# One layer of a hybrid block on one core: first-load blocks in unused tiles, the last gates' modulation inside the second norm, a branch projection ahead of two gates

## The chip, the core and the metric

The kernel runs on one core of a Trainium2 chip. The core has a matrix engine (TensorE, PE; its weight loads are shown as PEld), a vector engine (VectorE, DVE), an engine for activation functions (ScalarE, ACT), a general engine (GpSimd, POOL) and an engine that here only issues DMA transfers (SyncE, SP). They run side by side, each through its own list of instructions in order, and wait for one another by semaphores. The metric is the time on the device of one execution, in microseconds.

## What is computed

All in float32, batch 1: 512 latent tokens x, 256 context tokens ctx, width 1024. A vector c and a fixed vector c_ctx give six modulation vectors (shift, scale and gate for two halves of the layer) by one matrix of 1024 x 6144.

```python
mod_x = silu(c) @ w_mod + b_mod;  mod_c = silu(c_ctx) @ w_mod + b_mod
sh1, sc1, g1, sh2, sc2, g2 = split(mod, 6)          # latent ones; sh1, sc1 for the context too
h = rmsnorm(x, norm1_g) * (1 + sc1) + sh1           # context likewise
f, u, g = split(h @ w_in, [512, 1024])              # Fourier group, recurrent group, gate branch
u = dwconv(u)                                       # width 4, along rows
for d in (forward, backward):                       # context first, the latents go on from its end
    r, i = sigmoid(u @ w_a + b_a), sigmoid(u @ w_x + b_x)    # the "gates"
    a = exp(-8 * r * softplus(-lam))                # the "decays"
    s = scan(s * a + sqrt(1 - a * a) * (i * u))
rx = (s_fwd + s_bwd) * gelu(g)
mx = concat(rmsnorm(fourier(f)), rmsnorm(rx)) @ w_out
x = x + g1 * mx
h2 = rmsnorm(x, norm2_g) * (1 + sc2) + sh2
x = x + g2 * peer(h2)      # product-key retrieval over 16384 experts, top 16 of 8 heads
return rmsnorm(x, final_norm_g)
```

## The kernel before, in words

Tokens lie along the free dimension, channels along the 128 partitions. A float32 product is made of three matmuls of rounded halves (`mm3`, L131): high by high, high by low, low by high. Weights arrive in tiles `raw` of 128 x 2048 (1 MB), which are split by `split_w` (L126): ACT copies the high half (`whi`), DVE, or POOL where it says so, subtracts for the low half (`wlo`). There are two `raw` tiles and two more with the mark "U", and the same for the split weights; a load on SP waits until a tile of its kind is free. The other work tiles of the first part are 35 equal buffers (`bt`, 128 x 768), and the PSUM tiles are five "ps", two "pa" and one "pm".

PE, ACT and DVE follow the order in which the code is written, from the start of the kernel to the end of the first part: `in_order` (L83) chains all their instructions. On SP the loads of the opening are chained in the same way; POOL's order and SP's later one are the scheduler's, which may also place work of the second part early.

**Modulation.** The matrix comes in 24 loads (`mod_load`, L180); load n is multiplied by `mod_mm(n)` (L211), eight instructions into the PSUM tile "pm", which `cc32` (the two vectors) feeds as stationary operand. Loads 0 to 7 are reordered on the host so that 0 to 3 make the scale and 4 to 7 the shift of the first norm. `mod_first(z)` (L226) ends such a half: ACT copies the sums, PE turns them onto partitions by eight matmuls, DVE adds the bias. Loads 8 to 15 and 16 to 23 are each ended by `mod_out` (L239) in the same way; the last ones hold sc2 (`mods[:, 32:40]`) and g2 (`mods[:, 40:48]`). g2 is first needed late in the second part.

**Opening** (L183 to L335). SP loads x, blocks 0 to 3, the context, the first u weights, blocks 4 to 7, more weights. ACT squares the rows, PE sums them with ones (`mean_squares`, L256), `rsqrt` (L148) makes the root; blocks 0 to 3 give the scale, blocks 4 to 7 the shift. Then the u projection begins.

**Recurrence** (L465 to L538). For each of four channel blocks: convolution, `gates` (four products of the gate weights, ACT's sigmoids), `decays` (exponential, tanh, then a2 = a * a on POOL, L409, and a DVE instruction), `scans`. `gate_branch(k)` (L441) is the projection of the gate branch, 24 matmuls and a copy. `mod_cols(w)` (L458) loads block 8 + w and multiplies block 7 + w. After `gates(3)` follow `mod_cols(3)`, the Fourier weights' loads (L500), their splits, `mod_cols(4)` and (5), `decays([2])`, `gate_branch(3)` and the Fourier projection `f_mm`.

**Output loop** (L663 to L691). Eight blocks `out_mm(k)` of 24 matmuls; the first four take the Fourier half, the last four the recurrent half `mr`. `rec_norm` (L619) makes mr: a multiplication by the root on POOL (L621), ACT's high half and DVE's low half (`scaled_split`, L567). `out_add` (L634) evacuates; for k < 4 DVE makes a product (L641) and POOL adds it to x (L642), else DVE does both (L638). Each turn also multiplies one modulation block, 16 to 23, and `mod_out(2)` ends them at k = 7.

**Second norm** (L692 to L729). Squares of x are summed by PE (`x2_sums`), `rsqrt`, then new pools are opened where the first part's were: A2 from sc2, and for each of eight blocks a DVE product, ACT's high half and DVE's low half (`h2h`, `h2l`), which the query projection of the second part takes.

Of the kernel before, what the change touches and what calls it, by code (L numbers as in the profile page):

```python
# [14 lines left out]
AF = mybir.ActivationFunctionType  # L15
ALU = mybir.AluOpType

P = 128
# [3 lines left out]
ND = 8  # L22
# [29 lines left out]
def build(tc, xT, ctxT, c2t, vecs, wm, wu, wf, wg, wgate, wo, wq, keys, u, v, urow, vrow,  # L52
          dft, c64, sel, eye, out, dbg=None):
    nc = tc.nc
# [110 lines left out]
    def bt(dt=F32, n=L):  # L165
        return bp.tile([P, n], dt, tag="b", name="b")
# [7 lines left out]
    gel2 = p1c.tile([P, 1024], F32, name="gel2")  # L174
    cc32 = cpool.tile([P, ND, 32], F32, name="cc32")
    V.memset(cc32, 0.0)
    xn = [bt() for d in range(ND)]
    rawm = {}

    def mod_load(n, st=""):  # L180
        rawm[n] = load(wm[n // 8, n % 8], st)

    for d in range(ND):  # L183
        nc.sync.dma_start(x2[d], xT[d])
# [3 lines left out]
        nc.sync.dma_start(xn[d][:, :C], ctxT[d])  # L188
    rawu = {0: load(wu[0], cuts=2)}
    for n in range(4, 8):  # L190
        mod_load(n, ("U", "")[n % 2])
    rawu[1] = load(wu[1], "U")
    graw = load(wgate)
    in_order(first_load, (nc.sync.engine,))
# [15 lines left out]

    def mod_mm(n):  # L211
        t = rawm.pop(n)
        if n < 8:

            m, first, final = -1 - n // 4, n % 4 == 0, n % 4 == 3
            ds = [2 * (n % 4) + j // 2 for j in range(4)]
        else:
            m, first, final = n // 8, n % 8 == 0, n % 8 == 7
            ds = [n % 8] * 4
        if first:  # L220
            modp[m] = pst("pm")
        for j in range(4):
            PE.matmul(modp[m][32 * j:32 * j + 32], cc32[:, ds[j]], t[:, j * 512:(j + 1) * 512],
                      start=first, stop=final)

    def mod_first(z):  # L226

        sb = bt(F32, 512)
        act(sb, modp[-1 - z], AF.Copy)
        pT = pst("pa", 32)  # L230
        for b in range(4):
            PE.matmul(pT[:, 4 * b:4 * b + 4], sb[:, b * P:(b + 1) * P], vec[:, V_SEL2:V_SEL2 + 4], start=True, stop=True)
        pv = pT[:, :16].rearrange("p (b j z) -> p z j b", b=4, j=2)
        o = 8 - 8 * z
        for k, mm in enumerate((mods, modc)):
            V.tensor_tensor(mm[:, o:o + 8].rearrange("p (j b) -> p j b", j=2), pv[:, k],
                            vec[:, V_BMOD + o:V_BMOD + o + 8].rearrange("p (j b) -> p j b", j=2), op=ALU.add)

# [16 lines left out]

    def mean_squares(src, n, ss, ds):  # L256
        for d in ds:
            sq = bt()
            act(sq[:, :n], src[d], AF.Square)
            if n == T:  # L260
                if d % 2 == 0:
                    even = sq
                    continue
                V.tensor_tensor(sq[:, :n], sq[:, :n], even[:, :n], op=ALU.add)
            PE.matmul(ss[:, :n], ones, sq[:, :n], start=(d < 2 if n == T else d == 0), stop=(d == ND - 1))
# [20 lines left out]

    for n in range(4):
        mod_mm(n)
    mod_first(0)
    A1 = cpool.tile([P, 2, ND], F32, name="A1")  # L290
    for z, mm in enumerate((mods, modc)):
        V.scalar_tensor_tensor(A1[:, z], mm[:, 8:16], 1.0, vec[:, V_N1:V_N1 + 8], op0=ALU.add, op1=ALU.mult)
# [12 lines left out]
    wpu = [split_w(rawu[0], h) for h in range(2)]  # L305
    mod_mm(6)
    mod_mm(7)
    mod_first(1)

    parts = ((sc, modc), (sx, mods))  # L310

# [88 lines left out]
    def decays(ks):  # L400
        for k in ks:
            for dr in range(2):
                o = 4 * dr + k
                r = rr[k, dr]
                a = aa[k, dr] = bt()
                tact(a, r, AF.Exp, scale=n8[:, o:o + 1])
                tact(r, r, AF.Tanh, scale=z8[:, o:o + 1])
                a2 = bt()
                G.tensor_tensor(a2, a, a, op=ALU.mult)  # L409
                V.scalar_tensor_tensor(r, a2, 1.0, r, op0=ALU.add, op1=ALU.mult)  # L410

    def scans(ks):
# [78 lines left out]
    scans([0, 1])  # L491
    mod_cols(2)
    gate_branch(2)
    gates(2)
    gates(3)
    mod_cols(3)
# [17 lines left out]
    mod_cols(4, "U")  # L514
    mod_cols(5, "U")
    decays([2])
    gate_branch(3)
    f_mm(0, f0)
    f0 = f_weights(2)
    decays([3])  # L520
# [97 lines left out]

    def rec_norm(k):  # L619
        rx = hsum[k][:, C:]  # L620
        G.tensor_tensor(rx, rx, r, op=ALU.mult)  # L621
        mr.append(scaled_split(rx, vec[:, V_LG + k:V_LG + k + 1]))

    def out_mm(k, wp, ms):
# [38 lines left out]
    for k in range(8):  # L663
        psk[k] = out_mm(k, wpo[k], Ys if k < 4 else mr)
        if k == 1:
            ssf, ssr = pst("pa"), pst("pa")
            PE.matmul(ssf, ones, Y0, start=True, stop=True)
            PE.matmul(ssr, ones, sqr, start=True, stop=True)
            rF = bt(F32, 512)
            rsqrt(rF, bt(F32, 512), ssf, 512)  # L670
            r = bt(F32, 512)
            rsqrt(r, bt(F32, 512), ssr, 512)
            out_add(0, psk[0], rF)
        if k:
            out_add(k, psk[k], rF if k < 4 else None)
        if k > 4:
            x2_sums(k - 5)
        if k + 4 < 8:
            wpo[k + 4] = out_weights(k + 4)
        if 0 < k < 3:  # L680
            rec_norm(2 * k - 2)
            rec_norm(2 * k - 1)
        if k < 7:
            mod_cols(9 + k, "U")
        if k == 5:
            raw0 = load(wq[0])
        if k == 7:
            mod_mm(23)
            mod_out(2)
        if k == 6:  # L690
            wpq = [split_w(raw0, p, V) for p in range(2)]  # L691
    x2_sums(3)  # L692
    rsqrt(rstd2, bt(F32, 512), ss2[0], 1024)
    in_order(start, (PE.engine, S.engine, V.engine))
    if "x2" in dbg:
        for d in range(ND):
# [25 lines left out]
    for d in range(ND):  # L722
# [5 lines left out]
        V.scalar_tensor_tensor(lo, xn, shift, hi.bitcast(F32), op0=ALU.add, op1=ALU.subtract)  # L728
        h2.append((hi, lo))  # L729

    pt0.close()
    X2d = dpool.tile([ND, P, T], F32, name="X2d")
    for d in range(ND):
# [482 lines left out]
def prep(i):  # L1216
    a = {}
    a["xT"] = i["x"][0].T.reshape(ND, P, T)
    a["ctxT"] = i["ctx"][0].T.reshape(ND, P, C)
    cols = lambda z: z.reshape(-1, P).T  # L1220
    a["vecs"] = np.concatenate([cols(z) for z in (
        i["b_mod"][0], i["norm1_g"][0], i["norm2_g"][0], i["final_norm_g"], i["conv_w"][0],
        i["conv_b"][0], i["lru_b_a"][0], i["lru_b_x"][0], i["lru_lambda"][0],
        i["fourier_out_g"][0], i["lru_out_g"][0])]
                               + [np.eye(P, dtype=np.float32).reshape(P, 4, 32)[:, :, :2].reshape(P, 8)]
                               + [np.eye(P, dtype=np.float32).reshape(P, 2, 2, 32)[..., :2].sum(1).reshape(P, 4)], 1)
    a["c2t"] = np.stack([i["c"][0], i["c_ctx"]]).reshape(2, ND, P).transpose(2, 1, 0)
    wm = np.array(i["w_mod"][0].reshape(ND, P, 3, 2048).transpose(2, 0, 1, 3))
    wm[0] = (i["w_mod"][0][:, :2048].reshape(4, 2, P, 2, 1024)[:, :, :, ::-1]
             .transpose(3, 0, 2, 1, 4).reshape(ND, P, 2048))  # L1230
    a["wm"] = wm
    w = i["w_in"][0]
    st = lambda m: m.reshape(ND, P, 2, 2, P).transpose(2, 1, 3, 0, 4).reshape(2, P, 2048)
    a["wf"] = w[:, :512].reshape(2, 4, P, 512).transpose(0, 2, 1, 3).reshape(2, P, 2048)
    a["wu"] = st(w[:, 512:1024])
    a["wg"] = st(w[:, 1024:])
    gt = np.zeros((P, 2, 2, 2, 2, P), np.float32)
    for g, n in enumerate(("lru_w_a", "lru_w_x")):
        z = i[n][0].reshape(2, 2, 2, 2, 64, 64)
        for s in range(2):  # L1240
            gt[64 * s:64 * s + 64, :, :, g, :, 64 * s:64 * s + 64] = z[:, :, :, s].transpose(3, 1, 0, 2, 4)
    a["wgate"] = gt.reshape(P, 2048)
    a["wo"] = (i["w_out"][0].reshape(2, 4, P, 2, 4, P).transpose(0, 3, 2, 4, 1, 5)
               .reshape(4, P, 2048))
    a["wq"] = i["peer_w_q"][0].reshape(ND, P, 8, 2, P).transpose(2, 1, 3, 0, 4).reshape(8, P, 2048)
    a["keys"] = i["peer_sub_keys"][0].transpose(0, 3, 1, 2).reshape(8, P, 256)
    a["u"] = i["peer_u"][0].reshape(P, 64, 2, ND, P).transpose(1, 4, 2, 3, 0).reshape(64, P, 2048)
    a["v"] = (i["peer_v"][0].reshape(P, NG, JG, 4, 2, P).transpose(1, 3, 0, 4, 2, 5)
              .reshape(NG * 4, P, 2048))
    a["urow"] = i["peer_u"][0]  # L1250
    a["vrow"] = i["peer_v"][0]
    t = np.arange(T)[:, None]
    k = np.arange(256)[None]
    ang = 2 * np.pi * ((t * k) % T) / T
    z = np.stack([np.cos(ang), np.sin(ang)]).astype(np.float32)
    z[1, :, 0] = 1.0 - 2.0 * (np.arange(T) % 2)
    a["dft"] = z.reshape(2, 4, P, 256).transpose(2, 0, 1, 3).reshape(P, 2048)
    m = np.arange(64)
    ang = 2 * np.pi * ((m[:, None] * m[None]) % 64) / 64
    nrm = 1.0 / np.sqrt(512.0 * 64.0)  # L1260
    bd = np.zeros((2, P, P))
    for s in range(2):
        bd[0, 64 * s:64 * s + 64, 64 * s:64 * s + 64] = np.cos(ang) * nrm
        bd[1, 64 * s:64 * s + 64, 64 * s:64 * s + 64] = np.sin(ang) * nrm
    a["c64"] = np.stack([np.stack(hilo(bd[0])), np.stack(hilo(bd[1]))]).transpose(2, 0, 1, 3)
    a["sel"] = consts_sel()
    a["eye"] = np.eye(P, dtype=np.float32)
    return {n: np.ascontiguousarray(z) for n, z in a.items()}
# [30 lines left out]
```

## Time and profile before

| | |
|---|---|
| Runs | 1470.49 us median of 3 (1469.91 to 1470.79) |
| Profiled execution | 1473.89 us; its span, from first to last instruction, 1472.1 us |
| Busy share of the span | PE 94%, PEld 87%, DVE 84%, ACT 42%, POOL 46% |
| Mean granted clock of PE | 0.976 of full speed |

The first part, from the opening to the second norm, is the first sixth of the span. A row of the timeline gives the start and the length in us, the engine, the line, the operation, the tiles (written <- read), shapes, how often, and in brackets how long the engine stood idle before and what ended that. SPq is SP issuing a DMA. A merged row of several instructions (x4) gives the time from the first start to the last end. L70 is the line of the helper for activations, L115 that of the loads, L123 that of the low halves, L132 to L134 are `mm3`; the tiles tell them apart. "b" is any of the 35 buffers.

### The profile page before, as it was taken

Reading aid. Unit: us, or ns where it says so; the run is one execution under the profiler, and the core shown is the slowest. Engines: PE = TensorE matmul, PEld = TensorE weight load, DVE = VectorE, ACT = ScalarE, POOL = GpSimd, SP = SyncE. Lnnn points to the kernel's source line nnn. Section 1 sums busy time; section 2 is a strip of 40 time slices with the busy share of each in tenths; the row PEclk is TensorE's granted clock in tenths of the full one; section 3 lists DMA queues with packets and bytes.
Section 4 is the critical chain, followed back from the end, with each engine's and each line's share of the span. In section 5 each row is a group of like instructions: output and inputs, shape, how many; then the busy total and the mean of one; then the engine's idle time right before and its main releaser. Section 6 shows DMA issues by size and latency. Waiting matters only on the chain. (4 is left out here: it accounts for less than half of the span.)

```text
span 1472.1 us, 22568 instructions
## 1 busy us (share of the span) xinstructions
PE 1390.7 (94%) x8569; PEld 1287.3 (87%) x8569; DVE 1235.5 (84%) x2186; ACT 613.4 (42%) x881; POOL 680.6 (46%) x460
## 2 busy tenths in 40 slices
PE   6898998999989999999999999999999999899995
PEld 2775765888869999999999999999999999899995
DVE  5577875699988998488998989999898989899973
ACT  4467633443334656433333432424334343233351
POOL 0044163566430000365765757576675766545412
PEclk8899999999999999999999999999999999999998
DMA  9433446331226999999999998999999999999901
GB/s 336 159 114 143 172 172 237 116 132 62 78 88 222 314 304 307 347 371 367 400 361 416 343 388 336 405 365 399 397 365 364 406 351 414 392 410 398 391 32 55
DMA packets 130189, 420.61 MB, mean 286 GB/s; under 512 B 10400, under 2 KB 59808, under 8 KB 106016
## 3 DMA queue, kind: packets, MB, share of 16 engines
q1 hardware_dynamic: 83520, 251.03, 45.9%
q0 software_dynamic: 46560, 168.14, 29.8%
q8 instruction: 67, 1.10, 0.3%
q14 instruction: 42, 0.34, 0.1%
HBM read 385.41 MB, written 33.69 MB: 285 GB/s over the span
## 5 line engine op out<-in xcount | busy, mean ns | idle before, releaser
L70 ACT ACTIVATE whi<-raw 128x1024 fp32r<-128x1024 f32 x296 | 312.6, 1059 | 608.5 <-PE ps_pa L133 296.5
L123 DVE TENSOR_TENSOR wlo<-raw,whi 128x1024 fp32r<-128x1024 f32 x266 | 328.9, 1239 | 61.5 <-ACT whi L70 47.6
L132 PE MATMUL ps_pa<-h2h,whi 128*128 128x352 f32 x1024 | 335.1, 327 | 4.8 <-ACT act L70 4.8
L134 PE MATMUL ps_pa<-h2h,wlo 128*128 128x352 f32 x1024 | 334.3, 326 | 0.6 <-DVE wlo L123 0.6
L133 PE MATMUL ps_pa<-h2l,whi 128*128 128x352 f32 x1024 | 334.4, 327 | 0.0
L1086 POOL DMA_INDIRECT row<-vrow,eidx x128 | 196.2, 1533 | 131.6 <-DVE oacc L1107 93.5
L1086 POOL DMA_INDIRECT row<-urow,eidx x128 | 196.5, 1535 | 117.0 <-DVE row L1093 59.9
L133 PE MATMUL ps_ps<-wl,whi 128*128 128x352 f32 x640 | 207.5, 324 | 0.0
L134 PE MATMUL ps_ps<-wh,wlo 128*128 128x352 f32 x640 | 207.2, 324 | 0.2 <-DVE wlo L123 0.2
L132 PE MATMUL ps_ps<-wh,whi 128*128 128x352 f32 x640 | 206.6, 323 | 0.0
L132 PEld LDWEIGHTS ps_pa<-h2h,whi 128*128 128x128 f32 x1024 | 193.7, 189 | 6.9 <-ACT act L70 5.6
L134 PEld LDWEIGHTS ps_pa<-h2h,wlo 128*128 128x128 f32 x1024 | 193.3, 189 | 1.8 <-DVE wlo L123 0.9
L133 PEld LDWEIGHTS ps_pa<-h2l,whi 128*128 128x128 f32 x1024 | 193.5, 189 | 0.9
L1093 DVE SCALAR_TENSOR_TENSOR row<-row,hrow 128x1024 f32<-128x1024 f32 x128 | 154.1, 1221 | 33.4 <-DMA row<-urow,eidx 31.7
L1107 DVE SCALAR_TENSOR_TENSOR oacc<-row,gw,oacc 128x1024 f32<-128x1024 f32 x127 | 162.8, 1282 | 11.0 <-DMA row<-vrow,eidx 9.8
L134 PEld LDWEIGHTS ps_ps<-wh,wlo 128*128 128x128 f32 x640 | 120.6, 188 | 0.5 <-DVE wlo L123 0.5
L133 PEld LDWEIGHTS ps_ps<-wl,whi 128*128 128x128 f32 x640 | 120.5, 188 | 0.0
L132 PEld LDWEIGHTS ps_ps<-wh,whi 128*128 128x128 f32 x640 | 120.4, 188 | 0.0
L123 POOL TENSOR_TENSOR wlo<-raw,whi 128x1024 fp32r<-128x1024 f32 x30 | 72.0, 2402 | 84.8 <-ACT whi L70 56.9
L133 PE MATMUL ps_pa<-wl,whi 128*128 128x352 f32 x256 | 83.0, 324 | 0.0
L134 PE MATMUL ps_pa<-wh,wlo 128*128 128x352 f32 x256 | 82.8, 323 | 0.0
L132 PE MATMUL ps_pa<-wh,whi 128*128 128x352 f32 x256 | 82.7, 323 | 0.0
(299 smaller groups left out, 2606.7 us busy)
## 6 DMA issues: line engine op xcount, KB each, us to landing
raw<-u SPq DMA_DIRECT2D x64, 1024.0 KB
raw<-v SPq DMA_DIRECT2D x64, 1024.0 KB
raw<-wm SPq DMA_DIRECT2D x24, 1024.0 KB
Gd<-stg SPq DMA_DIRECT2D x22, 1024.0 KB
gt<-Gd SPq DMA_DIRECT2D x16, 1408.0 KB
raw<-wq SPq DMA_DIRECT2D x8, 1024.0 KB
Ad<-act SPq DMA_DIRECT2D x10, 704.0 KB
act<-Ad SPq DMA_DIRECT2D x10, 704.0 KB
```

Of the source, the lines that this page charges most:

```text
L70: return S.activation(o, i, f, **kw)
L123: lo_ins[0] = (lo_eng or V).tensor_tensor(dst[1], src, dst[0].bitcast(F32), op=ALU.subtract).ins
L132: PE.matmul(ps, a[0], b[0], start=start, stop=False)
L133: PE.matmul(ps, a[0], b[1], start=False, stop=False)
L134: PE.matmul(ps, a[1], b[0], start=False, stop=stop)
L1086: G.indirect_dma_start(out=t, out_offset=None, in_=tab, in_offset=bass.IndirectOffsetOnAxis(ap=e[:, s:s + 1], axis=0))
L1093: ins = V.scalar_tensor_tensor(t, t, 1.0, hr, op0=ALU.mult, op1=ALU.mult, accum_out=dt[:, s:s + 1])
L1107: ins = V.scalar_tensor_tensor(o, t, g[:, s:s + 1], o, op0=ALU.mult, op1=ALU.add)
```

## The change

Loads 4 to 7 get tiles of their own: sixteen buffers of the 35, of which 512 columns are used, are set aside before all others (`ahead`), and each load is four DMAs of 128 x 512 (`mod_load_b`). The squares of the first norm, which used such buffers, go into slices of `gel2`, a tile that is used later. Loads 16 to 23 are reordered like 0 to 7: 16 to 19 make sc2, 20 to 23 make g2. Loads 16 to 18 are multiplied in turns 0 to 2 of the output loop; 19 is multiplied and turned in turn 3; 20 to 23 are loaded in turns 3 and 4 into buffers of the 35, multiplied and turned behind the sums of the second norm, and their bias is added behind the eight blocks of h2. `mod_first` is split into `half_turned` (copy and turn) and `half_biased`. `gate_branch(3)` stands ahead of `gates(2)` and `gates(3)`. The squares of the decays and the multiplications in `rec_norm` go from POOL (G) to DVE (V).

```diff
+    ahead = {n: [bt()[:, :512] for j in range(4)] for n in range(4, 8)}
     xn = [bt() for d in range(ND)]
...
     def mod_load(n, st=""):
-        rawm[n] = load(wm[n // 8, n % 8], st)
+        t = load(wm[n // 8, n % 8], st)
+        rawm[n] = [t[:, j * 512:(j + 1) * 512] for j in range(4)]
+    def mod_load_b(n):
+        rawm[n] = ahead.get(n) or [bt()[:, :512] for j in range(4)]
+        for j, t in enumerate(rawm[n]):
+            nc.sync.dma_start(t, wm[n // 8, n % 8, :, j * 512:(j + 1) * 512])
...
     for n in range(4, 8):
-        mod_load(n, ("U", "")[n % 2])
+        mod_load_b(n)
...
     def mod_mm(n):
-        if n < 8:
+        if n < 8 or n >= 16:
...
-            PE.matmul(modp[m][32 * j:32 * j + 32], cc32[:, ds[j]], t[:, j * 512:(j + 1) * 512],
-                      start=first, stop=final)
+            PE.matmul(modp[m][32 * j:32 * j + 32], cc32[:, ds[j]], t[j], start=first, stop=final)
-    def mod_first(z):
+    def half_turned(n):
         sb = bt(F32, 512)
-        act(sb, modp[-1 - z], AF.Copy)
+        act(sb, modp[-1 - n // 4], AF.Copy)
         pT = pst("pa", 32)
         for b in range(4):
             PE.matmul(pT[:, 4 * b:4 * b + 4], sb[:, b * P:(b + 1) * P], vec[:, V_SEL2:V_SEL2 + 4], start=True, stop=True)
+        return pT[:, :16].rearrange("p (b j z) -> p z j b", b=4, j=2)
+    def half_biased(pv, o, outs):
+        for k, mm in enumerate(outs):
             V.tensor_tensor(mm[:, o:o + 8].rearrange("p (j b) -> p j b", j=2), pv[:, k],
...
     def mean_squares(src, n, ss, ds):
-            sq = bt()
+            sq = gel2[:, d % (1024 // n) * n:][:, :n]
...
-    mod_first(0)
+    half_biased(half_turned(3), 8, (mods, modc))
...
-    mod_first(1)
+    half_biased(half_turned(7), 0, (mods, modc))
...
-                G.tensor_tensor(a2, a, a, op=ALU.mult)
+                V.tensor_tensor(a2, a, a, op=ALU.mult)
...
     gate_branch(2)
+    gate_branch(3)
     gates(2)
     gates(3)
...
     decays([2])
-    gate_branch(3)
     f_mm(0, f0)
...
-        G.tensor_tensor(rx, rx, r, op=ALU.mult)
+        V.tensor_tensor(rx, rx, r, op=ALU.mult)
...
-        if k < 7:
+        if k < 3:
             mod_cols(9 + k, "U")
+        if k == 3:
+            mod_mm(19)
+            half_biased(half_turned(19), 32, (mods,))
+        if k in (3, 4):
+            mod_load_b(14 + 2 * k)
+            mod_load_b(15 + 2 * k)
         if k == 5:
             raw0 = load(wq[0])
-        if k == 7:
-            mod_mm(23)
-            mod_out(2)
...
     rsqrt(rstd2, bt(F32, 512), ss2[0], 1024)
+    for n in range(20, 24):
+        mod_mm(n)
+    last_gates = half_turned(23)
     in_order(start, (PE.engine, S.engine, V.engine))
...
         h2.append((hi, lo))
+    half_biased(last_gates, 40, (mods,))
...
-    wm[0] = (i["w_mod"][0][:, :2048].reshape(4, 2, P, 2, 1024)[:, :, :, ::-1]
-             .transpose(3, 0, 2, 1, 4).reshape(ND, P, 2048))
+    for m, o in ((0, -1), (2, 1)):
+        wm[m] = (i["w_mod"][0][:, 2048 * m:2048 * m + 2048].reshape(4, 2, P, 2, 1024)[:, :, :, ::o]
+                 .transpose(3, 0, 2, 1, 4).reshape(ND, P, 2048))
```

## Rows read from the trace of the kernel before

**Rows 1.** The waits of PE, 0 to 270 us: total, times, longest, in us.
```profile
PE ps_ps L132 <- ACT b L70: 8.8, 3, 7.3
```

**Rows 2.** The timeline of PE, 22 to 46 us: start, length, operation, [idle before].
```profile
25.41 6.72 PE L265 MATMUL ps_ps<-b,ones 128*128 128x256 f32 x16
...
35.00 1.06 PE L223 MATMUL ps_pm<-raw,cc 128*32 128x512 f32 x8 [1.02 <-DMA raw<-wm]
39.69 1.94 PE L223 MATMUL ps_pm<-raw,cc 128*32 128x512 f32 x8 [3.62 <-DMA raw<-wm]
```

**Rows 3.** The timeline of DVE, 24 to 46 us.
```profile
37.69 2.36 DVE L123 TENSOR_TENSOR wlo<-raw,whi 128x1024 fp32r<-128x1024 f32 x2
44.25 0.17 DVE L236 TENSOR_TENSOR mods<-ps_pa,vec 128x8 f32<-128x8 f32 x1 [4.21 <-PE ps_pa L232]
```

**Rows 4.** Busy time by stretch; the last two columns: DMA share, GB/s.
```profile
25.00:32.50 7.50, 7.50 (x23) 5.63 (x27) 5.79 (x12) 1.40 (x5) 0.00 (x0) 0.56 1.02 425
32.50:35.00 2.50, 1.49 (x16) 0.26 (x8) 2.19 (x6) 2.04 (x3) 0.00 (x0) 1.00 0.58 246
```

**Rows 5.** The DMA packets of 8 to 10 us.
```profile
DMA packets 404, 0.84 MB, mean 422 GB/s; under 512 B 49, under 2 KB 49, under 8 KB 385
```

**Rows 6.** The timeline of ACT, 100 to 136 us.
```profile
108.80 0.94 ACT L70 ACTIVATE b<-b,n 128x768 f32<-128x768 f32 x1 [1.64 <-DVE b L410]
...
117.16 1.28 ACT L70 ACT_TABLE_LOAD   x1 [0.18 <-DVE b L419]
118.45 3.33 ACT L70 ACTIVATE b<-ps_ps,vec 128x256 f32<-128x256 f32 x7
...
133.23 2.01 ACT L70 ACTIVATE whi<-raw 128x1024 fp32r<-128x1024 f32 x2 [5.19 <-DMA raw<-wf]
```

**Rows 7.** The timeline of DVE, 103 to 114 us.
```profile
104.24 0.96 DVE L410 SCALAR_TENSOR_TENSOR b<-b 128x768 f32<-128x768 f32 x1 [2.31 <-POOL b L409]
...
112.19 1.22 DVE L123 TENSOR_TENSOR wlo<-raw,whi 128x1024 fp32r<-128x1024 f32 x1
```

**Rows 8.** Busy time of PE on tile ps_pa in one stretch: us (instructions), granted clock.
```profile
103.40:109.20 5.80, 5.74 (x24) 1.00 0.89 347
```

**Rows 9.** The timeline of SP's DMA issues, 100 to 136 us.
```profile
128.37 1.19 SPq L115 DMA_DIRECT2D raw<-wf  x2
```

**Rows 10.** The timeline of DVE, 196 to 224 us.
```profile
202.66 2.72 DVE L641 SCALAR_TENSOR_TENSOR b<-ps_ps,mods,b 128x512 f32<-128x512 f32 x4
205.30 1.22 DVE L123 TENSOR_TENSOR wlo<-raw,whi 128x1024 fp32r<-128x1024 f32 x1
206.43 3.48 DVE L570 SCALAR_TENSOR_TENSOR b<-b,vec 128x512 fp32r<-128x512 f32 x2
```

**Rows 11.** The timeline of POOL, 200 to 224 us.
```profile
205.31 2.34 POOL L642 TENSOR_TENSOR x<-x,b 128x512 f32<-128x512 f32 x1
```

**Rows 12.** The timeline of ACT, 196 to 224 us.
```profile
212.35 0.72 ACT L70 ACTIVATE b<-b,vec 128x512 fp32r<-128x512 f32 x1 [2.23 <-POOL b L621]
212.98 1.04 ACT L70 ACTIVATE whi<-raw 128x1024 fp32r<-128x1024 f32 x1
```

**Rows 13.** The timeline of PE around 213 and from 240 to 253 us.
```profile
213.08 1.06 PE L223 MATMUL ps_pm<-raw,cc 128*32 128x512 f32 x8
...
242.21 1.06 PE L244 MATMUL ps_pa<-vec,b 128*128 128x8 f32 x8 [0.89 <-ACT b L70]
...
251.76 1.22 PE L132 MATMUL ps_ps<-h2h,whi 128*128 128x512 f32 x2 [5.82 <-ACT h2h L70]
```

**Rows 14.** The timeline of DVE, 244 to 250 us.
```profile
249.71 0.17 DVE L713 TENSOR_SCALAR A<-mods 128x8 f32<-128x8 f32 x1
```

**Rows 15.** The waits of SP, 195 to 262 us.
```profile
SPq L833 <- DVE h2l L728: 15.2, 1, 15.2
```

**Rows 16.** Busy time by stretch; third column from the right: granted clock.
```profile
250.00:251.00 1.00, 0.00 (x0) 0.00 (x0) 0.96 (x3) 0.01 (x1) 0.61 (x1) 0.50 0.00 0
256.00:257.00 1.00, 1.00 (x4) 0.78 (x3) 1.00 (x3) 0.93 (x2) 0.00 (x0) 0.59 0.00 0
```

More of the change, by code (lines that the diff above doesn't have):

```diff
@@ L232, in mod_first @@
             PE.matmul(pT[:, 4 * b:4 * b + 4], sb[:, b * P:(b + 1) * P], vec[:, V_SEL2:V_SEL2 + 4], start=True, stop=True)
-        pv = pT[:, :16].rearrange("p (b j z) -> p z j b", b=4, j=2)
-        o = 8 - 8 * z
-        for k, mm in enumerate((mods, modc)):
+        return pT[:, :16].rearrange("p (b j z) -> p z j b", b=4, j=2)
+    def half_biased(pv, o, outs):
+        for k, mm in enumerate(outs):
             V.tensor_tensor(mm[:, o:o + 8].rearrange("p (j b) -> p j b", j=2), pv[:, k],
```

## The prediction, made before the change was run

> **What bounds the kernel now.** I read the page first, then the waits of TensorE (PE) over the first 270 us, because only code of that stretch changes. PE has work for 94% of the span, so a microsecond counts only if it shortens PE's path. Its longest wait there is for ScalarE (ACT), 7.3 us once before the gates [rows 1]; the blocks of the first modulation load cost it up to 3.62 us at a time [rows 2], the second norm 5.82 [rows 13]. Then I read each stretch in order of time: its rows on every engine, its DMA rate and its granted clock. Behind the norm nothing is edited, and I carry any shift through unchanged. The sum is made in the profiled execution (span 1472.1 us, 1473.89 us with what lies around it); the median of the runs shown is 1470.49 us, 3.4 us less, and I apply the difference to that.
>
> **Opening.** Before, the last of the eight blocks reaches PE at 39.69 us, while the seventh was there at 35.00 [rows 2]. The DMA engines moved 425 GB/s up to 32.5 us and only 246 in the next 2.5 us [rows 4]: the eighth load had no free tile yet. With tiles of its own its megabyte follows the seventh's at 425 GB/s, 1.05 MB / 0.425 = 2.5 us, and reaches PE at about 37.5. It comes in quarters, so only the last quarter's multiplication is then left: I take 0.5 of the 1.94 us row. That is 38.0 against 39.69 + 1.94 = 41.63. The copy, the turn and the bias behind it shift with it. VectorE (DVE) is busy with the low halves of the weights until 37.69 + 2.36 = 40.05 and did the bias at 44.25 [rows 3]; it would now do it at 44.25 - 3.6 = 40.6, not held by them. Gain **3.6 us**; the bounds are 4.2 (DVE the limit) and the loss of rival 3.
>
> Quarters have rows of 2 KB. So have the x loads, and at 8 to 10 us, when 336 of 404 packets are between 2 and 8 KB, the rate is 422 GB/s [rows 5], with several transfers in flight. The Trainium skill (SBUF — State Buffer, The DMA setup-cost knee) puts one 256 KiB transfer at 224 GB/s and one of 1 MiB at about 341, for a fixed cost that each pays; it speaks against the cut. The 422 disagrees as long as transfers overlap; by the page's figure the opening would lose, as in rival 3.
>
> The squares of the first norm now go through two slots of a tile that is unused there (four for the context), so a square waits for the sum that read its slot. Bound: a 256-wide sum takes 6.72 / 8 = 0.84 us [rows 2], a 512-wide one twice that at the same clock, so some 3 us later in all at most. Cover: the multiplications by that root stand behind the bias of the first four blocks anyway. I take nothing; without the cover it is up to 3 us. The new tiles and the reordered weights cost nothing on the chip.
>
> **Decays and the branch projection.** Eight squares of the decays go from GpSimd (POOL) to DVE. A 768-wide operation costs DVE 0.96, and it stood idle 2.31 us before that row, waiting for POOL [rows 7]: no cost. ACT's 1.64 us stop at 108.80 [rows 6] goes, so what follows its exponentials comes 1.7 us sooner. The projection of branch 3 (24 matmuls, 5.74 us as its twin in [rows 8], 0.24 each) now runs inside PE's 7.3 us wait. Its second weight half, ready at 112.19 + 1.22 = 113.4 [rows 7], is ready at 111.7; 22 matmuls later it is 117.0. ACT evacuates it in its written order before the sigmoids: copy 0.6 (under the 0.72 of [rows 12]), table load 1.28, sigmoids at 118.9 against 118.45 [rows 6]. PE is now warm and starts the 48 gate matmuls (half of them 512 wide, half 256) at 117.0: 24 x 0.24 + 24 x 0.12 = 8.6, end 125.6. Before, they ended about one pass before 128.37 [rows 9], at 127.3.
>
> What is late next is the Fourier weights. Their load is issued at 128.37, when the modulation pass behind the gates frees a tile [rows 9]; ACT sits 5.19 us idle until they land at 133.23 [rows 6]. Before, the projection filled that for PE; now nothing does. The load moves only with the gates, 1.7 to 2.3 us. PE's new idle stretch of 4 to 5 us may halve its clock: in the norm it stands at half (1.2 of 2.4 GHz) after 4 us without work and is back only at about 256.8, 5 us after PE restarts [rows 13, 16], which loses 2.5 us. Sum: **gain 0.5 us** (bounds: gain 2.3, loss 0.8).
>
> **Output loop.** Modulation passes 20 to 23 (1.06 us each [rows 13]) leave the loop, 4.0 us of PE. In exchange pass 19 is turned inside the loop, at k = 3: PE does pass 19 (213.08 to 214.1 [rows 13]), waits for ACT's copy, turns, and only then goes on. PE, ACT and DVE run in written order, so the copy stands behind the high halves of the last two recurrent blocks and one weight split. Those high halves now wait for DVE, since rec_norm's four multiplications move there from POOL. Before, POOL ran ahead and the last high half came at 212.35 [rows 12].
>
> DVE's chain from 202.66 on, from [rows 10]: four evacuations 2.7, weight low half 1.2; then multiply 0.7, wait for ACT 0.8, low half 0.7, and this once more; two evacuations 1.4, weight low half 1.2; multiply, wait, low half, multiply. The last multiplication ends at 216.1 and ACT's high half at 216.9; with split 1.04 [rows 12] and copy 0.6 PE's turn starts at **218.6** at the earliest. That leaves POOL out. In [rows 11] a POOL add starts with DVE's 1.22 us low half of 205.30 and needs 2.34, ending 1.1 us behind it; DVE's next two low halves take 3.48 instead of 1.4 [rows 10]. They take turns, whole instructions at a time. Six POOL adds fall into DVE's new chain; placed one after the other they hold DVE 0.6, 1.25, 0.45, 0.65 and 1.25 us (one falls into a wait), and the turn starts at about **222.5**. The Trainium skill (SBUF — State Buffer, Who interferes with whom) has the same: a VectorE instruction with two SBUF inputs and a GpSimd one that reads SBUF block each other for the whole instruction. Without that rule it would be 218.6.
>
> So PE idles 4.5 to 8.4 us and its clock falls. The turn took 1.06 warm [rows 13], about 1.9 at half clock (as a pass: 1.94 for 1.06 [rows 2]): output block 4 starts at 220.5 to 224.4 instead of 214.1. From there to the last sum (251.76 - 5.82 = 245.94 [rows 13]) it was 31.8 us; less three passes (3.0) and the pass, wait and turn ahead of the sums (1.06 + 0.89 + 1.06 [rows 13]), 25.8, plus 1.3 for what of the 5 us at half clock is left: 247.6 to 251.5. The loop **loses** 1.7 to 5.6 us, its saved work included. I take 4.5, near the upper end, since [rows 10, 11] show the turns in this very stretch.
>
> **Norm.** Passes 20 to 23 (4.1 us) fill most of PE's 5.82 us wait, and ACT's copy is done before its first high half is due. But the first write into the new pools, A2, stood at 249.71 [rows 14], right behind the last reader of the old ones, and the key load waited 15.2 us for the last reader of a closed pool [rows 15]. If a new pool waits for all of the old, A2 waits for PE's turn at 4.1 + 0.9 + 1.06 = 6.1 us behind the sums instead of 3.8, and DVE's chain starts 2.3 us late. PE stays warm and gets some 2 of it back; the keys, which wait for the end of that chain, still come 0.5 to 1.8 us late. If pools wait tile by tile, the warm clock gains 2. I take a loss of **0.5**, nearer to the first. The 16 loads of these passes cost SP at most 0.6 us each [rows 9], some 20 us ahead of use: nothing. Behind them on SP wait the first query weights and ACT's split of those; that costs only if a tile isn't free.
>
> **Sum.** -3.6 - 0.5 + 4.5 + 0.5 = +0.9: 1471.4 us.
>
> **Rivals.**
> 1, as forecast: the new wait at k = 3 eats the gains. 1471.4, own range 1467.5 to 1475.
> 2, a short wait: POOL's adds fall into DVE's waits for ACT (loop +1.7) and pools wait tile by tile (-2): -3.6 - 0.5 + 1.7 - 2 = -4.4, 1466.1. For it: DVE's 0.8 us waits leave POOL room. Against: [rows 10, 11].
> 2b, the turn doesn't hold PE and the loop gives its 4.0: -3.6 - 0.5 - 4.0 + 0.5 = -7.6, 1462.9. Against it stands the written order.
> 3, slower: the quarters arrive late. The four blocks start at 27.6 (37.5 less four times 2.5); 4.2 MB at 346 GB/s end at 39.7 as before, which is where it decides. At 300 it is 41.6, and with the half multiplication saved the opening loses 0.4: 1475.4; at the 246 of [rows 4] it is 44.7: 1478.5. For it the skill's figure above, against it the 422.
>
> **How the numbers follow.** Chances: rival 1 0.46, 2 0.22, 2b 0.08, 3 0.24. 0.2% of this kernel is 2.9 us, about what a measurement can tell from no change. Faster: 0.18 of 2, 0.08 of 2b, 0.02 of 1, together 0.28. Slower: 0.21 of 3, 0.09 of 1, together 0.30. Same: 0.42. The range, 1464 to 1477, leaves out 2b and the far end of 3.
>
> **What would show it.** The last block at PE near 37.5 and the first projection near 41.5; the wait before the gates under 3 us and a new one before the Fourier matmuls; at k = 3 a PE wait of 4.5 to 8.4 us for ACT ahead of the turn, at half clock behind it; A2 behind PE's last turn. If that wait is under 2 us, or the blocks come after 39.7, the prediction is wrong.

## The result and the profile after

The changed kernel takes 1477.96 us (median of 5 runs, 1476.44 to 1481.40) against 1470.49 (5 runs, 1466.19 to 1473.04): ratio 1.0054, 95% interval 1.0032 to 1.0075, so some 8 us slower and not the 0.9 of the forecast, whose range ended at 1477. A second set of runs gave 1475.49 (4 runs) and 1.0039, 1.0020 to 1.0058. The profiled execution took 1477.81 us, span 1476.0.

What moved first, the opening. The timeline of PE and then of DVE (start, length, operation, [idle before]), against [rows 2, 3]:
```profile
28.94 10.65 PE L232 MATMUL ps_pm<-b,cc 128*32 128x512 f32 x32
40.28 1.05 PE L240 MATMUL ps_pa<-vec,b 128*128 128x4 f32 x8 [0.69 <-ACT b L70]
42.20 0.38 PE L132 MATMUL ps_ps<-b,whi 128*128 128x256 f32 x1 [0.87 <-ACT b L70]
```
```profile
38.21 2.35 DVE L123 TENSOR_TENSOR wlo<-raw,whi 128x1024 fp32r<-128x1024 f32 x2
41.37 0.17 DVE L245 TENSOR_TENSOR mods<-ps_pa,vec 128x8 f32<-128x8 f32 x1 [0.80 <-PE ps_pa L240]
```
The four passes of the second half run as one stretch and end at 39.59, not 38.0: PE follows the quarters as they land. The turn behind them takes 1.05 us, at full clock. The first projection starts at 42.20 (forecast 41.5; before 45.09, but 42.26 in a second execution, see `before_again`). The DMA packets of 27.6 to 38.5 us, the quarters, and of 11.3 to 21.2 us, mostly whole blocks of 1 MB:
```profile
DMA packets 2209, 4.31 MB, mean 396 GB/s; under 512 B 250, under 2 KB 250, under 8 KB 2160
```
```profile
DMA packets 1009, 4.06 MB, mean 410 GB/s; under 512 B 112, under 2 KB 571, under 8 KB 571
```
Around the gates the waits of PE, 104 to 136 us (total, times, longest), stand against [rows 1]: the 7.3 us are gone, and the Fourier weights are late next, as forecast.
```profile
PE ps_ps L132 <- ACT whi L70: 4.4, 1, 4.4
PE ps_pa L132 <- ACT whi L70: 1.3, 1, 1.3
PE ps_pa L134 <- DVE wlo L123: 0.7, 1, 0.7
```
Behind the 4.4 us the granted clock is 0.50 from 127 to 133 us, as the forecast feared; before, it was 0.53 from 119 to 124 us, behind the 7.3.

The output loop at k = 3, in the timelines of PE, ACT, DVE and POOL:
```profile
209.36 1.07 PE L232 MATMUL ps_pm<-raw,cc 128*32 128x512 f32 x8
218.03 1.87 PE L240 MATMUL ps_pa<-vec,b 128*128 128x4 f32 x8 [7.61 <-ACT b L70]
```
```profile
213.69 0.72 ACT L70 ACTIVATE b<-b,vec 128x512 fp32r<-128x512 f32 x1 [4.63 <-DVE b L630]
215.83 0.72 ACT L70 ACTIVATE b<-b,vec 128x512 fp32r<-128x512 f32 x1 [1.42 <-DVE b L630]
216.46 1.04 ACT L70 ACTIVATE whi<-raw 128x1024 fp32r<-128x1024 f32 x1
217.41 0.57 ACT L70 ACTIVATE b<-ps_pm 128x512 f32<-128x512 f32 x1
```
```profile
210.13 1.86 DVE L123 TENSOR_TENSOR wlo<-raw,whi 128x1024 fp32r<-128x1024 f32 x1
211.91 1.75 DVE L630 TENSOR_TENSOR b<-b 128x512 f32<-128x512 f32 x1
...
215.12 0.68 DVE L630 TENSOR_TENSOR b<-b 128x512 f32<-128x512 f32 x1
```
```profile
209.64 3.47 POOL L651 TENSOR_TENSOR x<-x,b 128x512 f32<-128x512 f32 x2 [3.44 <-DVE b L650]
```
Read them from the bottom. POOL's two adds run from 209.64 to 213.11; DVE's multiplication, which starts at 211.91 beside them, takes 1.75 us, and the same instruction takes 0.68 once POOL is idle. ACT's high half waits 4.63 us for that multiplication, which in DVE's order stands behind two evacuations and the low half of a weight. The copy of pass 19 is the last of ACT's rows, so PE idles 7.61 us ahead of the turn. The granted clock is in the third column from the right, of these stretches:
```profile
210.50:214.50 4.00, 0.00 (x0) 1.00 0.75 244
214.50:218.00 3.50, 0.00 (x0) 0.65 0.89 273
218.00:225.80 7.80, 7.76 (x22) 0.50 1.05 393
225.80:228.00 2.20, 2.20 (x11) 1.00 0.63 231
```
PE had been at 2.4 GHz; 5.1 us into the wait, at 215.5, it fell to 1.2 and stayed there for 7.7 us of work. In the second execution it fell 2.5 us into the same wait and stayed at 1.2 for 5.1 us of work. The norm, timelines of PE and DVE, against [rows 13, 14]:
```profile
245.67 1.13 PE L666 MATMUL ps_pa<-b,ones 128*128 128x512 f32 x2 [1.06 <-POOL b L669]
...
247.49 1.03 PE L664 MATMUL ps_pa<-b,ones 128*128 128x512 f32 x2
248.45 3.64 PE L232 MATMUL ps_pm<-b,cc 128*32 128x512 f32 x32
252.88 1.05 PE L240 MATMUL ps_pa<-vec,b 128*128 128x4 f32 x8 [0.80 <-ACT b L70]
256.30 1.08 PE L132 MATMUL ps_ps<-h2h,whi 128*128 128x512 f32 x2 [2.37 <-ACT h2h L70]
```
The 1.06 us ahead of the last sums are new. They come from POOL, where the add of the last squares stands behind the low half of a weight:
```profile
240.12 3.29 POOL L123 TENSOR_TENSOR wlo<-raw,whi 128x1024 fp32r<-128x1024 f32 x1 [0.65 <-ACT whi L70]
243.37 2.25 POOL L669 TENSOR_TENSOR b<-b 128x512 f32<-128x512 f32 x1
```
DVE in the norm:
```profile
251.45 0.69 DVE L154 SCALAR_TENSOR_TENSOR rstd<-b,rstd 128x512 f32<-128x512 f32 x1
254.13 0.17 DVE L728 TENSOR_SCALAR A<-mods 128x8 f32<-128x8 f32 x1 [1.99 <-DMA raw<-u]
```
The root is done at 252.14, but A2 comes at 254.13, right behind PE's turn (252.88 + 1.05 = 253.93). The profile names a load of the u table that happened to land then; the experiment `pool_free` shows that it is the turn.

### The profile page after: what moved, and what is told of

Its sections match the earlier page's. It is cut to its first block, busy times and chain, and to the rows that moved or that the text cites. A ratio compares the mean times of both kernels' runs of the same rounds, so it can differ in the third digit from the quotient of the medians.

```text
span 1476.0 us, 22643 instructions
## 1 busy us (share of the span) xinstructions
PE 1396.3 (95%) x8577; PEld 1289.4 (87%) x8577; DVE 1241.6 (84%) x2199; ACT 614.1 (42%) x882; POOL 666.2 (45%) x448
## 5 line engine op out<-in xcount | busy, mean ns | idle before, releaser
L1102 POOL DMA_INDIRECT row<-urow,eidx x128 | 200.9, 1569 | 114.9 <-DVE row L1109 61.9
```

The source lines that it names most:

```text
L1102: G.indirect_dma_start(out=t, out_offset=None, in_=tab, in_offset=bass.IndirectOffsetOnAxis(ap=e[:, s:s + 1], axis=0))
```

## The experiments

Theory A: the loss is in the output loop, where rec_norm's multiplications on DVE hold ACT's high halves and, behind them, the turn. Rival B: the turn inside the loop waits anyway. Rival C: the loss lies behind the loop. Times are medians of the runs, and each ratio is to runs of the kernel before in the same set, so a ratio and a difference of medians from two sets need not agree. Marks are from one profile each: "mark 1" is PE's first matmul behind the roots in the output loop (203.46 us before), "query" the first of the query projection (251.76 before), "mark 2" the first L883/L899 matmul behind PE's 3.7 us wait at the end of the search (409.43 before). The stretch between marks 1 and 2 has no row fetches, so it shows the edits without the differences of later stages; the clock still varies in it.

**One line undone (rec_pool).**
```diff
-        V.tensor_tensor(rx, rx, r, op=ALU.mult)
+        G.tensor_tensor(rx, rx, r, op=ALU.mult)
```


> The changed kernel with one line undone: the four multiplications of the recurrent blocks by their root run on POOL again. Theory A (the changed kernel loses its time in the output loop because those multiplications on DVE make ACT's high halves late, and the turn of pass 19 stands behind them in ACT's written order): the wait of PE ahead of that turn falls from 7.61 us to under 1.5, PE stays at full clock behind it, and with the 7.8 us at half clock (half of them lost, 3.9) the kernel is about 10 us faster than the changed one: 1466 to 1469. Rival B (the turn inside the loop waits whichever engine multiplies): the wait stays above 4 us and the time at 1475 to 1478. Rival C (the loss lies behind the loop, in the norm and the stages after it): the wait goes, but the time stays above 1472.


Measured 1467.26 us, ratio to the kernel before 0.9962 (0.9942 to 0.9981): 10.7 us faster than the changed kernel (8.2 by the second set's median, 11 to 14 by the ratios), and faster than the kernel before. The turn waits 0.78 us, and PE's timeline has matmuls of 0.39 us behind it (granted clock 1.00 from 213 to 230 us):
```profile
212.78 1.05 PE L240 MATMUL ps_pa<-vec,b 128*128 128x4 f32 x8 [0.78 <-ACT b L70]
...
214.01 0.39 PE L133 MATMUL ps_ps<-b,whi 128*128 128x512 f32 x1
```
Theory A stands; B falls, and so does C as the main cause. The one line takes away both the place of the multiplications in DVE's order and their meeting with POOL's adds; no run separates the two.

**The turn later (turn_late).**
```diff
         if k == 3:
             mod_mm(19)
+        if k == 5:
             half_biased(half_turned(19), 32, (mods,))
```


> The changed kernel with the turn of pass 19 put behind output block 5 instead of block 3; the multiplications stay on DVE. Theory A: no wait ahead of the turn any more, but output block 4 then waits itself for the high and low halves of recurrent blocks 2 and 3 (their last low half ended at 217.34 us in the changed kernel), 3 to 5 us of PE in all, so that only some 3 to 5 us come back: 1473 to 1475. Rival B (the turn alone is the cause): PE runs through, about 10 us faster than the changed kernel: 1466 to 1469. Rival C: the time stays above 1475.


Measured 1476.34 (1.0031, 1.0015 to 1.0047), less gain than theory A gave it, and far from B; the time is in the range of C, which rec_pool has ruled out. From mark 1 to the query 2.7 to 3.9 us came back. Output block 4 now waits for the same high halves itself, 3.4 us in all, and its matmuls again take 0.63 us instead of 0.39 behind that. In PE's timeline:
```profile
216.31 0.50 PE L132 MATMUL ps_ps<-b,whi 128*128 128x512 f32 x1 [2.50 <-ACT b L70]
217.10 0.50 PE L133 MATMUL ps_ps<-b,whi 128*128 128x512 f32 x1 [0.28 <-DVE b L579]
...
218.45 0.79 PE L132 MATMUL ps_ps<-b,whi 128*128 128x512 f32 x1 [0.62 <-ACT b L70]
...
220.25 0.63 PE L132 MATMUL ps_ps<-b,whi 128*128 128x512 f32 x1
```
So the place of the turn is the smaller part; the late high halves are the cause.

**Filling the wait (fill).**
```diff
             mod_mm(19)
+            idle = pst("pa")
+            for _ in range(7):
+                PE.matmul(idle, ones, Y0, start=True, stop=True)
```


> The changed kernel with seven extra matmuls of 512 columns whose result nobody reads between pass 19 and its turn (1.02 us each, 7.2 us in all), so that PE isn't idle while it waits there. If the half clock behind the wait costs what the rows show (218.0 to 225.8 us at half, so 3.9 us), the granted clock stays full and the time falls by 3 to 4 us, to about 1474, although PE does more work. Rival: the wait alone costs, the clock is of no account: 1477 to 1479.


Measured 1477.18 (1.0036, 1.0015 to 1.0056), a miss, and the time that the rival gave. The filler took 6.28 us, PE idled only 1.47 more, and the clock fell all the same, at 221.2, 1.3 us after PE had restarted, for 3.4 us. The two stretches, granted clock third from the right:
```profile
218.40:221.60 3.20, 1.73 (x12) 0.94 1.04 373
221.60:225.00 3.40, 3.40 (x11) 0.55 1.05 396
```
From mark 1 to the query it took 54.60 us against the changed kernel's 56.59 and 55.38 in two executions: between 0.8 and 2.0 us came back. That is what the clock gives back, against the rival's words: PE worked at half clock behind the wait for 7.7 us in the changed kernel, 5.1 in its second execution and 3.4 here. If half of that is lost (3.9, 2.6 and 1.7 us), mark 1 to the end of the last sum takes 44.9, 45.0 and 45.1 us without it, the same in all three, and 37.1 in rec_pool. The 7.9 us to rec_pool are the wait ahead of the turn (7.61 - 0.78) and the 1.06 us ahead of the last sums.

**The early edits alone (early_only):** opening, squares of the decays, branch projection; loop and norm as before.
```diff
+    ahead = {n: [bt()[:, :512] for j in range(4)] for n in range(4, 8)}
...
-                G.tensor_tensor(a2, a, a, op=ALU.mult)
+                V.tensor_tensor(a2, a, a, op=ALU.mult)
...
     gate_branch(2)
+    gate_branch(3)
     gates(2)
```


> The kernel before with the opening, the squares of the decays on DVE and the branch projection ahead of the two gates, and nothing of the output loop or the norm. At the entry of the output loop the changed kernel was 3.75 us ahead of the kernel before; if what is gained there is carried to the end, this one runs in 1466 to 1467.5. Rival C (the stages behind give or take some us whatever happened ahead of them, so that an early gain is lost): 1469 to 1472.


Measured 1469.14 (0.9981, 0.9966 to 0.9996), outside the expected range and in that of rival C. It goes from mark 1 to mark 2 in 206.07 us, the kernel before in 205.97: up to there what is gained early is carried, against rival C's mechanism. But it is 2 to 3 us (2.0 at mark 1 against the mean of two executions, 2.8 by the ratio) and not 3.75.

**The opening alone (open_only):** the first added line of the diff above, mod_load_b for blocks 4 to 7 and the squares in gel2.
```diff
...
-        mod_load(n, ("U", "")[n % 2])
+        mod_load_b(n)
...
```


> The kernel before with the opening alone (blocks 4 to 7 in quarters into tiles of their own, squares through two slots). Theory O (the quarters end at 38.5 us and the opening is worth little, since the last whole block of the kernel before landed anywhere between 37.5 and 39.7 us): 1 to 2 us faster than the kernel before, ratio 0.9985 to 0.9995. Rival, the prediction's term: 3.6 us faster, ratio 0.9975.


Measured 1468.83 (0.9989, 0.9973 to 1.0006), as Theory O expected. The interval, 4.0 us faster to 0.9 slower, doesn't exclude the term of 3.6 us; mark 1, 1.1 us ahead of the mean of two executions of the kernel before, speaks against it.

**The kernel before, again (before_again).** No edit.


> The kernel before, profiled a second time, to see which of its waits belong to one execution alone. If the wait of PE of 5.51 us at 1249.8 us and the start of the first projection at 45.09 us are chance, they move by microseconds here; the waits between 200 and 420 us should be the same within 0.1 us. Rival: both are the kernel's own and come again.


Measured 1470.60. In PE's timeline the last block and the first projection come 2.2 and 2.8 us earlier than in the first profile [rows 2], while the late wait came again, and those between 200 and 420 us are the same within 0.1:
```profile
37.52 1.30 PE L223 MATMUL ps_pm<-raw,cc 128*32 128x512 f32 x8 [2.48 <-DMA raw<-wm]
...
42.26 0.58 PE L132 MATMUL ps_ps<-b,whi 128*128 128x256 f32 x1 [0.87 <-ACT b L70]
...
1254.86 0.66 PE L133 MATMUL ps_pm<-wl,whi 128*128 128x352 f32 x1 [5.18 <-DVE wl L123]
```
So the 39.69 of [rows 2], on which the opening's term was built, is one execution's. Here the passes end at 37.52 + 1.30 = 38.82, 0.8 us ahead of the changed kernel's first execution.

**The changed kernel, again (after_again).** No edit.


> The changed kernel, profiled a second time. If its losses between 200 and 470 us are its own, the wait ahead of the turn is 7.6 us again within 0.1, the clock is at half behind it again, and from the entry of the output loop to 470 us it again takes some 10 us more than the kernel before; only the opening and the stage behind 900 us move. Rival: the 10 us are one execution's bad luck with the clock.


The wait ahead of the turn is 7.62 us; marks 1 to 2 take 213.73 us (215.59 the first time, 205.97 and 206.29 before). The clock is at half again behind the wait, for 5.1 us of work. The loss is the kernel's own, 7.4 to 9.6 us; "some 10" was the upper end.

**The passes back in the loop (norm_in_loop),** on rec_pool.
```diff
+        if k > 3:
+            mod_mm(16 + k)
+        if k == 7:
+            half_biased(half_turned(23), 40, (mods,))
...
-    for n in range(20, 24):
-        mod_mm(n)
-    last_gates = half_turned(23)
...
-    half_biased(last_gates, 40, (mods,))
```


> rec_pool with passes 20 to 23 back in the output loop, one behind each of output blocks 4 to 7, and their turn behind block 7. Theory N (filling the norm's wait with the passes is worth its 4 us in the loop, less about 2 us for A2, which then stands behind PE's turn): this kernel is 2 to 4 us slower than rec_pool (1467.3), 1469 to 1471, with PE's wait in the norm at 5.8 us again and A2 0.1 to 0.2 us behind the last instruction of the root. Rival P (the passes in the norm are worth nothing, because A2's delay and PE's clock take it all back): within 1 us of rec_pool.


Measured 1471.21 (0.9988, 0.9964 to 1.0013), 0.0026 of the ratio above rec_pool, 3.8 us, as Theory N expected; PE's wait in the norm is 5.9 us again. The two intervals overlap, but marks 1 to 2 take 4.4 us more than in rec_pool (209.13 against 204.72). Passes 20 to 23 in the norm are worth having.

**A copy tile outside the closing pool (pool_free),** on rec_pool; `half_turned` takes the tile as an argument.
```diff
...
-    last_gates = half_turned(23)
+    last_gates = half_turned(23, wspl.tile([P, 1024], F32R, tag="whiU", name="whi")[:, :512].bitcast(F32))
```


> rec_pool with the tile of the last turn's copy taken from the pool of the weight splits, which stays open, in place of the pool that is closed behind the loop; the passes read tiles of the closing pool as before. If A2 waits for every reader of the closing pool, it now waits for pass 23 alone (242.03 us in rec_pool's trace) and comes about 0.1 us behind the root's last instruction in place of 2.04; the query projection starts some 1.9 us sooner: 1465 to 1466. Rival: A2 waits for something else (the profile names the landing of a load): 2.0 us of wait stay and the time is rec_pool's 1467.


A2 comes as expected, in DVE's timeline, and then this; the last row is POOL's in the same stretch:
```profile
241.13 0.69 DVE L154 SCALAR_TENSOR_TENSOR rstd<-b,rstd 128x512 f32<-128x512 f32 x1
242.01 0.17 DVE L728 TENSOR_SCALAR A<-mods 128x8 f32<-128x8 f32 x1 [0.19 <-PE ps_pm L232]
...
242.42 4.19 DVE L741 SCALAR_TENSOR_TENSOR sq<-x,A,rstd 128x512 f32<-128x512 f32 x3
```
```profile
243.60 2.46 POOL L123 TENSOR_TENSOR wlo<-raw,whi 128x1024 fp32r<-128x1024 f32 x1 [0.45 <-ACT whi L70]
```
A2 did wait for PE's turn; now it comes right behind pass 23, the last reader that is left in the closing pool. Mark 1 to query falls from 44.98 to 43.07 us, the 1.9 expected; the time, 1469.19 with ratio 0.9961 (0.9932 to 0.9990), does not move. POOL's split of a weight half now meets DVE's first three multiplications, which take 4.19 us (2.08 in the changed kernel), and PE waits 1.6 us for a low half and 1.9 for the keys.

**The Fourier weights sooner (wf_early),** on rec_pool.
```diff
+    mod_cols(3)
     gates(2)
     gates(3)
-    mod_cols(3)
```


> rec_pool with modulation pass 10 ahead of gates 2 and 3 in place of behind them, so that its weight tile is free some 8 us sooner and the Fourier weights are loaded sooner. If PE's new wait of 4.35 us before the Fourier matmuls is the wait for that load alone, it falls under 1.5 us and the time by 3 us: 1464. Rival: pass 10's own weights aren't there so early, PE waits ahead of the gates instead, and nothing is gained: 1467.


Measured 1468.38 (0.9970, 0.9946 to 0.9994): nothing gained. The first of the two loads is issued at 113.85 in place of rec_pool's 124.44, the second only at 123.44, and PE waits 3.5 and 1.5 us in place of 4.3 and 0.5. In ACT's timeline the high halves stand behind sigmoids, and four of these now wait for a scan on DVE:
```profile
124.74 2.00 ACT L70 ACTIVATE b<-ps_ps,vec 128x256 f32<-128x256 f32 x4 [3.74 <-DVE b L433]
126.61 2.02 ACT L70 ACTIVATE whi<-raw 128x1024 fp32r<-128x1024 f32 x2
```
The rival's result, by another wait than it named. That mark 1 comes 2.3 us ahead of rec_pool's in this profile is mostly not the edit: from 40 to 50 us, long before it, the granted clock is 1.00 here and 0.85 and 0.81 in the two halves of that stretch in rec_pool, where half clock costs 1.7 us.

**All of them together (best):** rec_pool with the edits of turn_late, pool_free and wf_early.


> rec_pool with the turn of pass 19 behind output block 5, the tile of the last turn's copy in the pool that stays open, and pass 10 ahead of gates 2 and 3. If the waits that these take away add up (0.8 us ahead of the turn, 1.9 in the norm, about 0.5 ahead of the Fourier matmuls), it is 3 us faster than rec_pool, ratio to the kernel before about 0.994. Rival: what each frees is taken back by the next wait (VectorE held by a POOL subtraction, half clock behind 390 and 410 us), and it stands where rec_pool stands, at 0.996.


Measured 1466.90 (0.9975, 0.9958 to 0.9991). It is faster than the kernel before and the changed one, but not clearly different from rec_pool, whose interval overlaps: the rival holds.

The marks side by side, from PE's timelines:

| kernel | mark 1 | query | mark 2 | 1 to query | 1 to 2 |
|---|---|---|---|---|---|
| before | 203.46 | 251.76 | 409.43 | 48.30 | 205.97 |
| before_again | 202.56 | 250.84 | 408.85 | 48.28 | 206.29 |
| after | 199.71 | 256.30 | 415.30 | 56.59 | 215.59 |
| after_again | 201.36 | 256.74 | 415.09 | 55.38 | 213.73 |
| early_only | 201.00 | 249.28 | 407.07 | 48.28 | 206.07 |
| open_only | 201.88 | 250.11 | 408.16 | 48.23 | 206.28 |
| rec_pool | 201.32 | 246.30 | 406.04 | 44.98 | 204.72 |
| turn_late | 201.54 | 254.26 | 413.20 | 52.72 | 211.66 |
| fill | 201.52 | 256.12 | 414.75 | 54.60 | 213.23 |
| norm_in_loop | 201.83 | 252.72 | 410.96 | 50.89 | 209.13 |
| pool_free | 201.10 | 244.17 | 406.50 | 43.07 | 205.40 |
| wf_early | 199.03 | 244.01 | 403.42 | 44.98 | 204.39 |
| best | 202.16 | 244.94 | 405.53 | 42.78 | 203.37 |

Mark 1 varies by up to 2 us between executions with the same edits ahead of it (199.71 and 201.36 in the changed kernel). Half of PE's time at half clock between the first projection and mark 1 is 2.0 us in the first of these and 4.5 in the second.

## Why the prediction was wrong, point by point

Most mechanisms were right. Three terms and the stretch behind the norm, put at nothing, were mis-sized, all in one direction; one mechanism, PE's warm clock in the norm, failed.

**Opening, -3.6.** This is the step that was furthest off. It set the new chain against "39.69 + 1.94", a block that landed 2.2 us earlier in the second profile, and it let the quarters follow at 425 GB/s; they came at 396. Open_only gained 1.6 us by its ratio (-4.0 to +0.9), and reaches mark 1 at 201.88, 1.1 us ahead of the mean of the two executions of before (203.01). Rival 3, late quarters, was half right: the passes ended at 39.59, between the forecast's 38.0 and the 41.63 before, and behind the 38.82 of before_again. The squares' slots cost nothing at the end, as forecast: PE's first sums ran later, DVE's low halves ended 0.5 us later (38.21 + 2.35 = 40.56), and the bias at 41.37 was waiting for PE.

On the page that was weighed there (the Trainium skill, SBUF — State Buffer, The DMA setup-cost knee): the trace has 396 GB/s in quarters and 410 for whole blocks. The measurement lies far from the page's 224 GB/s for one transfer of 256 KiB, and a few per cent below whole blocks; with several transfers in flight the cut cost little.

**Decays and branch projection, -0.5.** Right, as far as one profile of open_only shows. The waits before the gates are 1.3 and 0.7 us (forecast under 3), and the Fourier weights are late instead (4.4 us), with half clock behind that wait as forecast. The eight profiles with all early edits and nothing else there (wf_early and best left out) reach mark 1 at 201.17 on the mean, 0.7 us before open_only. Both early terms together: -1.8, not -4.1.

**Output loop, +4.5.** The wait (forecast 4.5 to 8.4) is 7.61, its place and cause are as forecast, and rec_pool shows it: with one line back on POOL the wait and the half clock behind it are gone. From mark 1 to the end of the last sum it was 245.94 - 203.46 = 42.48 us before and 248.52 - 199.71 = 48.81 after; in after_again the last sum ended at 248.96, 47.60 us: +6.3 and +5.1. Too low was the clock's part: 0.8 for the turn and "1.3 for what of the 5 us at half clock is left" were counted, and half of the time at half clock is 3.9 us in the first execution (7.7 us at half) and 2.6 in the second (5.1 us, the length that was forecast). Not foreseen was 1.06 us: the last sums wait for a POOL add that stands behind a weight's low half on POOL. DVE's chain as listed in the forecast adds up to 216.5, not 216.1, which moves nothing. That the turn came at 218.03 although the forecast had 222.5 with POOL is no contradiction: the loop began 3.75 us sooner. A multiplication took 1.75 us beside POOL's adds and 0.68 alone. The Trainium skill (SBUF — State Buffer, Who interferes with whom) has these two block each other for whole instructions; the trace agrees.

**Norm, +0.5.** The sign of A2 was right (2.0 us behind the root; pool_free takes it away). The step that failed is "PE stays warm and gets some 2 of it back". PE idled 0.80 and 2.37 us, and the clock, full until then, fell as it restarted (in the second execution shortly before):
```profile
256.30:259.10 2.80, 2.80 (x8) 0.53 0.01 2
```
From the last sum's end to the query it is 7.78 us in both executions (256.30 - 248.52; 256.74 - 248.96) against 5.82: +2.0. Behind the query PE then worked at half clock for 3.4 and 5.6 us, against 4.8 and 5.8 in the two executions of before: of the 2 us some 0.4 came back on the mean.

**Behind the norm, "I carry any shift through unchanged".** Wrong by 0.5 to 1.3 us up to mark 2: query to mark 2 takes 159.00 and 158.35 us against 157.67 and 158.01. PE's wait for the key split is 1.57 us in both executions, 1.05 before; that is the 0.5, and the term had it under the norm as the keys' lateness. The rest is the clock, which varies: behind that wait it is at half for 3.4 us in the first execution and full in the second. A long stretch at half clock there is rec_pool's, behind a wait of 3.44 us that every kernel has; first rec_pool, then early_only, both from the end of that wait:
```profile
388.53:396.00 7.47, 7.47 (x30) 0.56 0.43 155
```
```profile
390.97:398.50 7.53, 7.53 (x39) 0.77 0.43 154
```

**The sum.** -1.8 + 5.7 + 2.0 + 0.9 = +6.8 (the first from the eight profiles, the others means of the two executions), against +0.9 forecast and ratios of 1.0054 and 1.0039 (+7.9 and +5.7 us). Of the 5.9 us of error the opening with the decays has 2.3, the norm 1.5, the loop 1.2 and the stages behind 0.9. The two profiled executions differ by only 3.9 us (1477.81 - 1473.89): at mark 2 they were 5.9 apart, and later, in the stage with the row fetches, 2 us of that came back; 1.8 did in the second executions. PE's waits for DVE from 1200 to 1300 us are 7.1 us before and 4.9 after in the first pair, which would explain it, but 5.2 and 6.2 in the second, so the cause stays open. So does why the same wait is followed by half clock for a longer time in one execution than in another, and how the wait at k = 3 divides between DVE's order and POOL's adds.

## What to carry to other kernels

An operation that runs ahead on an engine of its own is not free to move: on an engine that works in written order it stands behind waits that it didn't have, and everything that waits for it moves too. Before putting a matmul that needs another engine's copy into a written order, find what stands ahead of that copy on its engine. And price a load by its arrival in more than one execution; one profile's late megabyte is no saving.

## What the runs showed of the hardware

A stretch of useless matmuls did not spare PE the half clock: in fill PE worked 6.28 of the 7.75 us ahead of the turn and still was at 0.55 of full clock from 221.6 to 225 us. Three executions with nearly the same wait (7.61, 7.62 and 7.75 us, the last one filled) ran at half clock behind it for 7.7, 5.1 and 3.4 us, and half of these times is the whole difference between them in that loop, within 0.2 us. The same wait of 3.44 us was followed, over 7.5 us, by 0.56 of full clock in one kernel and 0.77 in another. And beside a POOL instruction of 2.46 us with operands in SBUF three DVE multiplications took 4.19 us in place of 2.08.
